# Splitting 8 KB weight tiles in one piece instead of two halves, with three buffers for each part

## The chip, the cores and the metric

The kernel runs on one core of a Trainium2 chip. The metric is the device time of one execution in microseconds, the median of three runs; lower is better.

## The reference, cut to what matters

The reference is two transformer-like blocks in float32 for one sequence of 256 tokens with 2048 channels. The first block computes six modulation vectors from a condition (`silu(c) @ w_ada + b_ada`), normalises and projects x, runs a state-space mixer and a dilated attention side by side, projects back, and adds a gated feed-forward layer. The second block has a neighbourhood attention, a latent attention, an attention over 256 memory tokens, and another feed-forward layer.

```python
mod = silu(c) @ w_ada + b_ada                    # 2048 -> 6 x 2048
proj = modulate(rms(x)) @ w_in                   # 256x2048 @ 2048x4096
x = x + gate1 * (concat(y_ssm, y_att) @ w_out)
x = x + gate2 * (silu(h2 @ w_gate) * (h2 @ w_up)) @ w_down
...
x = x + memory_attention(rmsnorm(x), rmsnorm(mem), w_xq, w_xk, w_xv, w_xo)
x = x + (silu(h @ w_gate_2) * (h @ w_up_2)) @ w_down_2
```

For the change only this matters: nearly all the work is products of 256 rows of activations with large float32 weight matrices, and each weight is used once.

## The kernel before, in words

**Weight tiles.** All weights come from HBM in tiles of 1 MB: 128 partitions by 4 chunks by 512 columns, 8 KB on each partition (four tiles have only 320 columns). `Flow.order` is a list, written out when the program is built, of all tiles in the order in which they are used. A tile of kind "w" is a matmul weight; a tile of kind "a" is a piece of `w_ada`. `Flow.run` walks the list. `feed` keeps up to six tiles ahead in the raw buffers `r` (L198, L199, issued from SyncE's queue). SyncE waits there until the VectorE work that last read the buffer is done.

**An "a" tile** is handed to `s_ada` (L948): one VectorE instruction of 128x2048 multiplies it by the condition and sums. There are 96 of them, mixed into the first part of the list, about one for each "w" tile at first and two for three later, until near 900 us.

**A "w" tile** is split in `split_half` into a part `h`, rounded to the matmul's format (fp32r) by a ScalarE copy (L207), and the rest `l = r - h` by a VectorE subtraction (L208). Before the change this is done for each half of a tile: two copies and two subtractions of 128x1024, into four buffers of 4 KB for `h` and four for `l`, so that two tiles fit. The argument `shared` would put the subtraction on GpSimd; `share` is `(0,)` everywhere, so it never does.

**The product** of a tile is in `mm3`: for each half, eight matmuls of 128x512 that use only `h` (L221 and L222, alternating), then four that use `l` (L226). So a tile is 24 matmuls, and TensorE needs the first `l` eight matmuls after the first `h`. `group` makes a loop of these over the tiles that add up in one accumulator, and hands the accumulator to a `done_*` task at its end.

**The order of the instructions** is that of the program text; nothing is reordered. Each engine executes its own instructions in that order. With two tiles split, `run` sends the older to `main` (its matmuls are issued) and then calls `step`, which advances every open task by one piece: evictions of accumulators (L875, L1227 on ScalarE, L871 and others on VectorE), transposes and further splits of activations (L262 to L264, L271 to L275), the state-space parameters and sections (L468 to L750), attention heads (L1090 to L1103), statistics (L291). So on each engine the order is: split of tile n+1, matmuls of tile n, tasks, split of tile n+2, matmuls of tile n+1, tasks. An "a" tile's L948 stands where the list has it, between two splits.

```python
split.append([])
for i in range(2):
    split[-1].append(k.split_half(r, i, ...))
    n += 1
    if n == k.NW:
        main.send(split.pop(0))
        self.step()
        n -= 2
```

Of the kernel before, what the change touches and what calls it, by code (L numbers as in the profile page):

```python
# [10 lines left out]
F32 = mybir.dt.float32  # L11
F32R = mybir.dt.float32r
AF = mybir.ActivationFunctionType
OP = mybir.AluOpType
# [136 lines left out]
class Core:  # L151
    NU = 40
    NU2 = 15
    NR, NW = 6, 4

    def __init__(self, ctx, tc):
        self.tc, self.nc = tc, tc.nc
        nc = self.nc

        def pool(name, **k):  # L160
            return ctx.enter_context(tc.tile_pool(name=name, bufs=1, **k))

        self.cp, self.wp, self.up, self.sp = pool("cp"), pool("wp"), pool("up"), pool("sp")
        self.pp = pool("pp", space=PSUM)
        self.dp = pool("dp", space=DRAM)
        self.n = 0
        self.ident = self.const([128, 128], "ident")
        make_identity(nc, self.ident)
        self.ones = self.const([128, 128], "ones")
        nc.gpsimd.memset(self.ones, 1.0)  # L170
        self.mhalf = self.const([128, 8], "mhalf")
        nc.gpsimd.memset(self.mhalf, -0.5)
# [26 lines left out]
        self.nc.sync.dma_start(r, src)  # L199
        return r  # L200

    def split_half(self, r, i, shared):

        nc = self.nc
        h, l = [self.wp.tile([128, 2, r.shape[-1]], F32R, name=self.nm(n), tag=n, bufs=self.NW) for n in "hl"]
        r = r[:, 2 * i:2 * i + 2]
        nc.scalar.activation(h, r, AF.Copy)  # L207
        (nc.gpsimd if shared else nc.vector).tensor_tensor(l, r, h.bitcast(F32), op=OP.subtract)  # L208
        return h, l

    def mm3(self, ps, acts, parts, first, last, ts=(0, 1)):

# [132 lines left out]
class Flow:  # L345


    def __init__(self, k):
        self.k = k
        self.order, self.fed, self.loaded = [], 0, []  # L350
        self.tasks = []
        self.ready = []
        self.lead = None
        self.share, self.nth = (0,), 0

    def add(self, task, rate=1):
        self.tasks.append([task, rate, 0.0])
# [25 lines left out]
    def run(self, main, other):  # L383

        k = self.k
        next(main)
        for g in other.values():
            next(g)
        split, n = [], 0
        for kind, _ in self.order:  # L390
            self.feed(k.NR)
            r = self.loaded.pop(0)
            if kind != "w":
                other[kind].send(r)
                continue
            split.append([])
            for i in range(2):
                split[-1].append(k.split_half(r, i, i >= 2 - self.share[self.nth % len(self.share)]))
                n += 1
                if n == k.NW:  # L400
                    main.send(split.pop(0))
                    self.step()
                    n -= 2
            if self.lead is not None:
                self.lead = next(self.lead, None) and self.lead
            self.nth += 1
        try:
            for p in split:
                main.send(p)
                self.step()  # L410
        except StopIteration:
            pass
        self.until(lambda: not self.tasks)
# [342 lines left out]
def build(ctx, tc, A, out):  # L756
    nc = tc.nc
    V, S, G, PE, SY = nc.vector, nc.scalar, nc.gpsimd, nc.tensor, nc.sync
    ctx.enter_context(tc.manual_schedule())
    k = Core(ctx, tc)  # L760
    fl = Flow(k)
# [84 lines left out]
    def group(acts, done, kbs, key=None, first=True, last=True, half=None):  # L846


        ps = open_ps.pop(key) if not first else [k.pm(), k.pm()] if half else k.pg()
        for i, kb in enumerate(kbs):  # L850
            parts = yield
            fl.until(lambda: kb in acts)
            end = last and i == len(kbs) - 1
            for ts in ((0,), (1,)) if half and end else ((0, 1),):
                for j in range(2):
                    k.mm3(ps, acts[kb][2 * j:2 * j + 2], parts[j], first and i == 0 and j == 0,
                          end and j == 1, ts)
                if half and end:
                    half(ps[ts[0]], ts[0])
        if half:  # L860
            return
        if last:
            fl.add(done(ps))
        else:
            open_ps[key] = ps
# [64 lines left out]
    def vals(g):  # L930
        def done(ps):
            o = tok(ps, r_mem)
            yield
            for t in range(2):
                SY.dma_start(mv[g][:, t], o[t])
        return done
# [51 lines left out]
    def s_norm1():  # L988
        for _ in range(6):
            yield  # L990
        for g in R4:
            load_x(g)
            yield
            yield
        for _ in range(4):
            yield
        for g in R4:
            row_stats(x[g], ss1, g)
            yield
        k.row_rstd(ss1, r1)  # L1000
        yield
        for g in R4:
            xs = scaled(g, r1)
            x[g] = [None, None]
            while (0, g // 2) not in got or (1, g // 2) not in got:
                yield
            acts1[g] = modulate(xs, g, 0)
            yield
# [122 lines left out]
    def s_prep():  # L1131
        yield from ssm.params()
        for s in range(NSEC):
            yield from ssm.prep(s)
        for _ in range(3):
            yield
        ssm.finish()
# [398 lines left out]
    def main():  # L1536
        prep = fl.add(s_prep(), 1)
        fl.add(s_norm1())
        yield from group(m_acts, keys(0), R4)
        fl.share = (0,)  # L1540
        prep[1] = 2
        for g in (1, 2, 3):
            yield from group(m_acts, keys(g), R4)
        for g in R4:
            yield from group(m_acts, vals(g), R4)
        m_acts.clear()
        fl.share = (0,)
        prep[1] = 3
        fl.add(s_run())
        fl.add(s_heads1())  # L1550
        done = {"u": done_u, "q": done_q, "k": done_k, "v": done_v}
        for n, g in EARLY:
            yield from group(acts1, hold((n, g % 2)), (0, 1))
        for n, g in EARLY:
            yield from group(acts1, done[n](g % 2), (2, 3))
        for n, g in LATE:
            yield from group(acts1, done[n](g % 2), R4)
        acts1.clear()
        for g in R4:
            yield from group(mixed_acts, out1(g, 0), (2,))  # L1560
        fl.share = (0,)
        for g in range(2):
            yield from group(glu_acts, done_glu(g), (0, 1))
        glu_acts.clear()
        for g in R4:
            yield from group(mixed_acts, out1(g, 1), (3,))
        for g in R4:
            yield from group(mixed_acts, out1(g, 2), (0, 1), half=(lambda ps, t: out1_end(3, ps, t)) if g == 3 else None)
        fl.until(lambda: not fl.tasks)
        ssm_scope.close()  # L1570
        pool2.append(ctx.enter_context(tc.tile_pool(name="pool2", bufs=1)))
        rope.append(pool2[0].tile([128, 2, 2, 32], F32, name="rope"))
        S.dma_start(rope[0], A["rope"].rearrange("p (a b c) -> p a b c", a=2, b=2))
        fl.share = (0,)
        fl.add(norm2())
        yield from ffn(acts2, None, fin1)
        acts2.clear()
        yield from group(acts3, done_cq, R4)
        yield from group(acts3, done_ckv, R4)
        fl.add(s_na())  # L1580
        fl.add(s_mla())
        for n in range(3):
            yield from group(acts3, done_qkv(n, 0), R4)
        for i in range(2):
            parts = yield
            fl.until(lambda: "ckv" in lat)
            for g in range(2):
                ps = k.pg()
                k.mm3(ps, lat["ckv"], parts[g], True, True)
                fl.add(done_ukv(i, g)(ps))  # L1590
        for g in (0, 2, 1):
            yield from group(cq_acts, done_uq(g), (0,))
        for n in range(3):
            yield from group(acts3, done_qkv(n, 1), R4)
        acts3.clear()
        for i in (1, 0):
            for g in R4:
                yield from group(y_acts, out2(i, g), (2 * i, 2 * i + 1))
        for g in R4:
            yield from group(acts4, done_xq(g), R4)  # L1600
        acts4.clear()
        seen = set()
        for g, kbs in XO:
            last = 3 in kbs
            yield from group(x_acts, out3(g), kbs, g, g not in seen, last)
            seen.add(g)
        x_acts.clear()
        for g in R4:
            fn.append(unit2())
            S.dma_start(fn[g], A["fnorm"][:, 512 * g:512 * g + 512].to_broadcast([128, 512]))  # L1610
        yield from ffn(acts5, r5, fin2, half2)
# [23 lines left out]
```

## Time and profile before

| | |
|---|---|
| median of 3 runs | 2713.08 us (2709.04 to 2713.55) |
| the profiled execution's own time | 2711.92 us |
| its span, first to last instruction | 2710.1 us |
| TensorE busy (matmuls) | 2616.3 us, 97% |
| VectorE busy | 1670.5 us, 62% |
| ScalarE busy | 1269.8 us, 47% |
| mean granted TensorE clock | 0.989 of full speed |

The page says what each engine did in one execution. A share over the whole span averages over stages that have different limits, so the rows below are mostly of stretches. In the rows PE is TensorE, DVE VectorE, ACT ScalarE, SP SyncE, and L208 is line 208 of the kernel before.

### The profile page before, as it was taken

What the parts mean: (1) busy time and instruction counts of PE and PEld (TensorE: products, weight loads), DVE (VectorE), ACT (ScalarE), POOL (GpSimd) and SP (SyncE); (2) the same over time, 40 slices, a digit from 0 to 9 for tenths busy, and PEclk for the clock granted to TensorE, in tenths of its full rate; (3) what the DMA queues carried; (4) which work ended last, traced back from release to release, by engine and by line L of the source; (5) the groups of instructions that cost most, each with busy time, mean ns of one, the idle gap of its engine ahead of it and who ended that gap; (6) DMA issues with size and microseconds to landing.
All of it is one profiled execution on the core that took longest, in us unless ns stands there. A gap on an engine that the chain in (4) does not pass through costs nothing.

```text
span 2710.1 us, 31194 instructions
## 1 busy us (share of the span) xinstructions
PE 2616.3 (97%) x12144; PEld 2171.3 (80%) x12144; DVE 1670.5 (62%) x2124; ACT 1269.8 (47%) x1818; POOL 98.6 (4%) x103
## 2 busy tenths in 40 slices
PE   8889989888999999999999999999999999999998
PEld 6778777776877888888888878888888888888887
DVE  7987999878766554554465454655554544455445
ACT  5465446553644344433445554555544433443434
POOL 2000000100000000000000021100000000000001
PEclk9999999999999999999999999999999999999999
DMA  8988765667676555555545434454455555555552
GB/s 348 362 289 328 307 244 215 253 225 297 256 277 232 200 196 190 186 194 195 186 168 192 171 130 162 166 200 171 178 215 197 186 189 196 191 186 186 187 198 96
DMA packets 90147, 578.98 MB, mean 214 GB/s; under 512 B 10000, under 2 KB 12432, under 8 KB 22672
## 3 DMA queue, kind: packets, MB, share of 16 engines
q1 hardware_dynamic: 80928, 561.61, 55.8%
q10 hardware_dynamic: 9072, 15.38, 1.7%
q8 instruction: 95, 1.56, 0.2%
q14 instruction: 52, 0.43, 0.0%
HBM read 570.67 MB, written 6.29 MB: 213 GB/s over the span
## 4 chain that ended last, share of the span: by engine, by line
PE 79%; DVE 15%; ACT 2%; issue 2%; DMA 1%; POOL 0%; ACTq 0%; DVEq 0%; POOLq 0%
PE g L226 24%; PE g L221 24%; PE g L222 24%; DVE l L208 4%; DVE r L948 4%; PE m L238 2%; DVE v L627 1%; ACT h L207 1%; DVE C L635 0%; PE m L342 0%; PE m L1484 0%; PE m L1471 0%; DVE u L732 0%; PE m L240 0%; PE m L226 0%
## 5 line engine op out<-in xcount | busy, mean ns | idle before, releaser
L208 DVE TENSOR_TENSOR l<-r,h 128x1024 fp32r<-128x1024 f32 x866 | 1028.5, 1223 | 573.6 <-ACT h L207 568.0
L221 PE MATMUL g<-h,u 128*128 128x512 f32 x3424 | 1352.6, 395 | 8.8 <-ACT h L207 6.5
L222 PE MATMUL g<-h,u 128*128 128x512 f32 x3424 | 1338.2, 391 | 0.0
L207 ACT ACTIVATE h<-r 128x1024 fp32r<-128x1024 f32 x866 | 884.1, 1056 | 625.1 <-PE g L222 593.0
L226 PE MATMUL g<-l,u 128*128 128x512 f32 x3424 | 922.2, 391 | 33.0 <-DVE l L208 33.0
L226 PEld LDWEIGHTS g<-l,u 128*128 128x128 f32 x3424 | 643.2, 189 | 178.3 <-DVE l L208 45.6
L221 PEld LDWEIGHTS g<-h,u 128*128 128x128 f32 x3424 | 647.9, 189 | 144.8 <-ACT h L207 10.2
L222 PEld LDWEIGHTS g<-h,u 128*128 128x128 f32 x3424 | 648.0, 189 | 132.4 <-issue 1.0
L948 DVE CUSTOM_DVE_ANT_0 r<-r,cond,vec 128x2048 f32<-128x2048 f32 x96 | 224.5, 2343 | 0.2
L271 ACT ACTIVATE u<-m 128x512 fp32r<-128x512 f32 (+1 forms) x80 | 42.7, 574 | 164.1 <-PE m L238 128.3
L272 DVE TENSOR_TENSOR u<-m,u 128x512 fp32r<-128x512 f32 (+1 forms) x80 | 50.0, 658 | 86.6 <-ACT u L271 86.5
L291 ACT ACTIVATE j<-u 128x512 bf16<-128x512 f32 (+2 forms) x92 | 47.3, 514 | 118.2 <-DVE u L1204 31.2
L238 PE MATMUL m<-ident,u 128*128 128x128 f32 x372 | 53.4, 287 | 19.8 <-POOL base_e L488 7.1
L274 ACT ACTIVATE u<-m,vec 128x256 fp32r<-128x256 f32 x86 | 38.9, 472 | 69.8 <-PE m L342 30.8
L275 DVE SCALAR_TENSOR_TENSOR u<-m,vec,u 128x256 fp32r<-128x256 f32 x86 | 40.0, 481 | 48.2 <-ACT u L274 48.1
L238 PEld LDWEIGHTS m<-ident,u 128*128 128x128 f32 x372 | 45.9, 148 | 27.5 <-ACT u L978 8.7
L299 POOL TENSOR_TENSOR r<-s,mhalf 128x2 f32<-128x2 f32 x5 | 5.5, 1102 | 1098.7 <-DVE s L298 1098.7
L1251 DVE TENSOR_TENSOR w<-g,w 128x512 f32<-128x512 f32 x24 | 16.5, 687 | 43.1 <-PE g L226 43.1
L1235 DVE SCALAR_TENSOR_TENSOR w<-g,r,w 128x512 f32<-128x512 f32 x22 | 15.5, 747 | 44.4 <-PE g L226 44.4
L1233 DVE TENSOR_TENSOR w<-g,w 128x512 f32<-128x512 f32 x22 | 14.2, 686 | 44.3 <-PE g L226 44.3
L1507 DVE TENSOR_TENSOR u<-g,u 128x512 f32<-128x512 f32 x22 | 14.2, 686 | 44.3 <-PE g L226 44.3
L1227 ACT ACTIVATE w<-g,r 128x512 f32<-128x512 f32 x22 | 13.9, 686 | 52.9 <-PE g L226 52.9
(238 smaller groups left out, 1204.6 us busy)
## 6 DMA issues: line engine op xcount, KB each, us to landing
r<-in_w_ada_dram SPq DMA_DIRECT2D x96, 1024.0 KB, 5.6
r<-in_wg_dram SPq DMA_DIRECT2D x88, 1024.0 KB, 4.8
r<-in_wu_dram SPq DMA_DIRECT2D x88, 1024.0 KB, 4.8
r<-in_wd_dram SPq DMA_DIRECT2D x88, 1024.0 KB, 4.8
r<-in_w_in_dram SPq DMA_DIRECT2D x32, 1024.0 KB, 6.0
r<-in_w_out_dram SPq DMA_DIRECT2D x32, 1024.0 KB, 4.8
r<-in_w_qkv_dram SPq DMA_DIRECT2D x24, 1024.0 KB, 4.8
r<-in_w_xk_dram SPq DMA_DIRECT2D x16, 1024.0 KB, 9.0
```

Source lines behind the costliest of these rows:

```text
L207: nc.scalar.activation(h, r, AF.Copy)
L208: (nc.gpsimd if shared else nc.vector).tensor_tensor(l, r, h.bitcast(F32), op=OP.subtract)
L221: nc.tensor.matmul(ps[t][:, :n], al[:, s], h[:, k], start=first and k == 0, stop=False)
L222: nc.tensor.matmul(ps[t][:, :n], ah[:, s], h[:, k], start=False, stop=False)
L226: nc.tensor.matmul(ps[t][:, :n], ah[:, s], l[:, k], start=False, stop=last and k == len(acts) - 1)
L238: self.nc.tensor.transpose(o, i, self.ident)
L271: nc.scalar.activation(h, ps, AF.Copy)
L272: nc.vector.tensor_tensor(l, ps, h.bitcast(F32), op=OP.subtract)
L274: nc.scalar.activation(h, ps, AF.Copy, scale=w)
L275: nc.vector.scalar_tensor_tensor(l, ps, w, h.bitcast(F32), op0=OP.mult, op1=OP.subtract)
L291: self.nc.scalar.activation(j[:, :n], src, AF.Square, accum_out=acc)
L948: V.tensor_tensor_reduce(r, r, cond, 1.0, v("b_ada", 8 * h + j), OP.mult, OP.add, md[h // 2][:, n:n + 1])
```

## The change

A tile is split whole: one ScalarE copy and one VectorE subtraction of 128x2048. `h` and `l` have three buffers of 8 KB each, where they had four of 4 KB. The two halves that `mm3` uses are slices of the whole tile, so the order of the matmuls is as before. `run` sends the older tile when two are split, at the same place as before. The unused `share` and `nth` go, and the scratch for GpSimd's descriptors is made smaller.

```diff
-    NR, NW = 6, 4
+    NR, NH, NL = 6, 3, 3
...
-    def split_half(self, r, i, shared):
+    def split_tile(self, r):
 
         nc = self.nc
-        h, l = [self.wp.tile([128, 2, r.shape[-1]], F32R, name=self.nm(n), tag=n, bufs=self.NW) for n in "hl"]
-        r = r[:, 2 * i:2 * i + 2]
+        h, l = [self.wp.tile([128, 4, r.shape[-1]], F32R, name=self.nm(n), tag=n, bufs=b)
+                for n, b in (("h", self.NH), ("l", self.NL))]
         nc.scalar.activation(h, r, AF.Copy)
-        (nc.gpsimd if shared else nc.vector).tensor_tensor(l, r, h.bitcast(F32), op=OP.subtract)
-        return h, l
+        nc.vector.tensor_tensor(l, r, h.bitcast(F32), op=OP.subtract)
+        return [(h[:, i:i + 2], l[:, i:i + 2]) for i in (0, 2)]
...
-            split.append([])
-            for i in range(2):
-                split[-1].append(k.split_half(r, i, i >= 2 - self.share[self.nth % len(self.share)]))
-                n += 1
-                if n == k.NW:
-                    main.send(split.pop(0))
-                    self.step()
-                    n -= 2
+            split.append(k.split_tile(r))
+            if len(split) == 2:
+                main.send(split.pop(0))
+                self.step()
...
-    nc = bacc.Bacc("TRN2", target_bir_lowering=False, num_devices=1, dynamic_dma_scratch_size=512)
+    nc = bacc.Bacc("TRN2", target_bir_lowering=False, num_devices=1, dynamic_dma_scratch_size=128)
```

## Rows read from the trace of the kernel before

**Rows 1.** The page, chain that ended last: shares of the span by engine.

```profile
PE 79%; DVE 15%; ACT 2%; issue 2%; DMA 1%; POOL 0%; ACTq 0%; DVEq 0%; POOLq 0%
```

**Rows 2.** Busy us by stretch: PE, PEld, DVE, ACT, POOL, then PEclk, DMA share, GB/s.

```profile
27.00:173.00 146.00, 132.48 (x604) 105.20 (x602) 141.93 (x273) 71.63 (x112) 9.40 (x6) 1.00 0.93 345
270.00:515.00 245.00, 221.29 (x1156) 186.52 (x1155) 236.91 (x455) 123.49 (x262) 17.66 (x10) 0.95 0.66 251
580.00:656.00 76.00, 66.51 (x286) 52.26 (x285) 75.86 (x87) 32.92 (x50) 0.00 (x0) 0.98 0.85 320
750.00:1400.00 650.00, 646.30 (x2892) 534.25 (x2891) 351.41 (x338) 274.26 (x310) 0.00 (x0) 1.00 0.55 202
```

**Rows 3.** The same columns (no POOL), only instructions on accumulator tile g.

```profile
750.00:1400.00 650.00, 635.90 (x2788) 522.08 (x2787) 26.62 (x40) 10.71 (x20) 1.00 0.55 202
```

**Rows 4.** Timeline, VectorE and TensorE, 112 to 119 us: start, length, engine, line.

```profile
112.57 2.34 DVE L948 CUSTOM_DVE_ANT_0 r<-r,cond,vec 128x2048 f32<-128x2048 f32 x1
114.84 2.35 DVE L208 TENSOR_TENSOR l<-r,h 128x1024 fp32r<-128x1024 f32 x2
...
116.11 1.19 PE L226 MATMUL g<-l,u 128*128 128x512 f32 x4 [1.93 <-DVE l L208]
```

**Rows 5.** Waits of TensorE, 0 to 1000 us: us in total, times, longest.

```profile
PE g L226 <- DVE l L208: 32.6, 28, 3.4
...
PE g L221 <- ACT h L207: 6.5, 4, 2.8
```

**Rows 6.** Groups by form, whole span: busy us, mean ns | idle before, releaser.

```profile
L208 DVE TENSOR_TENSOR l<-r,h 128x1024 fp32r<-128x1024 f32 x858 | 1022.4, 1226 | 571.3 <-ACT h L207 567.5 <-DMA r<-in_w_out_dram 0.8
L948 DVE CUSTOM_DVE_ANT_0 r<-r,cond,vec 128x2048 f32<-128x2048 f32 x96 | 224.5, 2343 | 0.2
...
L208 DVE TENSOR_TENSOR l<-r,h 128x640 fp32r<-128x640 f32 x8 | 6.2, 822 | 2.3 <-PE g L226 1.7 <-ACT h L207 0.5
...
L207 ACT ACTIVATE h<-r 128x1024 fp32r<-128x1024 f32 x858 | 878.7, 1059 | 622.6 <-PE g L222 590.5 <-DMA r<-in_w_in_dram 11.1 <-DMA r<-in_w_xk_dram 8.5
```

**Rows 7.** Line 208 in three stretches (27, 270 and 580 us): count, ns min/median/max.

```profile
L208 DVE TENSOR_TENSOR l<-r,h x44: 1215/1218/1224, 26.1 to 170.3; 128x1024 fp32r<-128x1024 f32 x44
...
L208 DVE TENSOR_TENSOR l<-r,h x55: 1211/1218/1226, 269.7 to 514.5; 128x1024 fp32r<-128x1024 f32 x55
...
L208 DVE TENSOR_TENSOR l<-r,h x22: 1210/1218/1223, 583.1 to 655.6; 128x1024 fp32r<-128x1024 f32 x22
```

**Rows 8.** Timeline of ScalarE, 7 to 11 us: an activation of 128x2048.

```profile
8.25 1.91 ACT L894 ACTIVATE cond<-cond 128x2048 f32<-128x2048 f32 x1 [5.31 <-DMA cond<-in_c_dram]
```

**Rows 9.** Chain that ended last, around 410, 653 and 371 us: start, length, what.

```profile
409.92 0.95 ACT h L207
...
410.90 2.36 DVE l L208 x2
...
653.06 0.96 ACT h L207
...
654.07 0.50 PE g L221
...
370.40 1.15 DVE l L208
...
371.59 2.07 PE g L226 x4
```

**Rows 10.** Timeline, 1929 to 1936 us: ScalarE, VectorE, TensorE.

```profile
1931.90 1.99 ACT L207 ACTIVATE h<-r 128x1024 fp32r<-128x1024 f32 x2
...
1932.97 2.36 DVE L208 TENSOR_TENSOR l<-r,h 128x1024 fp32r<-128x1024 f32 x2 [1.96 <-ACT h L207]
...
1934.94 1.07 PE L226 MATMUL g<-l,u 128*128 128x512 f32 x4
```

**Rows 11.** Waits of ScalarE and VectorE, 0 to 750 us: us in total, times, longest.

```profile
ACT h L207 <- PE g L222: 46.9, 33, 3.5
...
DVE l L208 <- ACT h L207: 22.3, 20, 3.8
```

More of the change, by code (lines that the diff above doesn't have):

```diff
@@ L353, in __init__ @@
         self.lead = None
-        self.share, self.nth = (0,), 0
     def add(self, task, rate=1):
@@ L388, in run @@
             next(g)
-        split, n = [], 0
+        split = []
         for kind, _ in self.order:
@@ L395, in run @@
                 continue
-            split.append([])
-            for i in range(2):
-                split[-1].append(k.split_half(r, i, i >= 2 - self.share[self.nth % len(self.share)]))
-                n += 1
-                if n == k.NW:
-                    main.send(split.pop(0))
-                    self.step()
-                    n -= 2
+            split.append(k.split_tile(r))
+            if len(split) == 2:
+                main.send(split.pop(0))
+                self.step()
             if self.lead is not None:
                 self.lead = next(self.lead, None) and self.lead
-            self.nth += 1
         try:
@@ L1539, in main @@
         yield from group(m_acts, keys(0), R4)
-        fl.share = (0,)
         prep[1] = 2
@@ L1546, in main @@
         m_acts.clear()
-        fl.share = (0,)
         prep[1] = 3
@@ L1560, in main @@
             yield from group(mixed_acts, out1(g, 0), (2,))
-        fl.share = (0,)
         for g in range(2):
@@ L1573, in main @@
         S.dma_start(rope[0], A["rope"].rearrange("p (a b c) -> p a b c", a=2, b=2))
-        fl.share = (0,)
         fl.add(norm2())
```

## The prediction

> **What bounds the kernel now.** I read the chain of waits first, since the busy shares mislead: TensorE is busy 97% of the span, but the chain gives it 79% and VectorE 15% [rows 1]. The table by stretch shows where that 15% lies. From 27 to 173 us VectorE is busy 141.93 of 146 us, from 270 to 515 us 236.91 of 245, from 580 to 656 us 75.86 of 76 [rows 2]. These stretches, 467 us together, go at VectorE's pace: for each weight tile it has one subtraction pair, mostly one L948, and tasks. From 750 to 1400 us TensorE is busy 646.3 of 650 us and VectorE about half [rows 2]; there a matmul of an accumulator takes 635.90 / 2788 = 0.228 us [rows 3], a tile of 24 about 5.5 us, and nothing that only VectorE or ScalarE saves can shorten it.
>
> The timeline shows how TensorE waits in the first kind of stretch: VectorE ends an L948, starts the pair at 114.84, and TensorE's first l matmul comes at 116.11, one half (1.2 us) later, after 1.93 us of idling [rows 4]. Up to 1000 us there are 28 such waits, 32.6 us together, and four for h, 6.5 us [rows 5].
>
> **The parts of the change, and what each costs.** The sum is made against the profiled execution's own 2711.92 us (span 2710.1), which is 1.2 us below the median of 2713.08. About 0.2%, 5.4 us, is what a measurement of this kernel can tell from no change.
>
> *One subtraction instead of two.* The trace has no subtraction of 128x2048. The two forms of L208 give a line: (1226 - 822) / 384 = 1.052 ns for a column [rows 6], so 1226 + 1024 x 1.052 = 2303 ns, near the 2343 ns of L948, which also reads two inputs of 128x2048 [rows 6]. A pair takes 2.35 us in the timeline [rows 4], not 2 x 1.226, because the second starts before the first has been written. So a tile saves 2.36 - 2.30 = 0.06 us of VectorE's time. That counts only where VectorE sets the pace: 44 + 55 + 22 = 121 halves, 60 tiles [rows 7], so 60 x 0.06 = 3.6 us are gained. The ends: at L948's price 0.01 us a tile and 1 us in all; at the bare slope, 2048 x 1.052 = 2.15 us, 0.2 us a tile and 12 us in all. I take the line through the same instruction's two sizes. The other tiles save the same behind TensorE, at no gain; TensorE's 5.5 us for a tile cover 2.3.
>
> *One copy instead of two.* An activation of 128x2048 takes 1.91 us [rows 8], a pair 1.99 [rows 10]: 0.08 us less for ScalarE, which is near half busy everywhere in [rows 2]. I take nothing for that. But h is now ready 1.91 us after the copy starts, and was ready for its first half after 1.06 [rows 6]: 0.85 us later. That costs where the chain goes from a first copy at once into VectorE or TensorE, as at 409.92 and 653.06 [rows 9]. I count six such places in the chain up to 656 us, at 279, 410, 434, 444, 539 and 653 us (the two shown stand for them): 6 x 0.85 = 5.1 us lost. At the low end ScalarE's queue has let it start earlier and nothing is lost; before these copies ScalarE came straight from other work, so I take the whole.
>
> *The first l comes with the second.* It is ready 2.30 us after the subtraction starts, and was after 1.226: 1.07 us later. In a stretch at VectorE's pace TensorE only waits longer at the first l and no longer behind it, and VectorE, which paces both, does not notice. The lateness is paid once, where the chain leaves VectorE by a first half for TensorE, as 370.40 to 371.59 [rows 9]; I find it again at 513: 2 x 1.07 = 2.1 us. The low end is nothing; the high end is the first rival.
>
> *Late in the kernel*, where TensorE sets the pace, a late part costs only what its slack doesn't cover. At 1931.90 the copy starts, h would end at 1933.81, l at 1936.11, and TensorE reads l at 1934.94: 1.2 us late [rows 10]. Four other places after 1400 us come out 0.5 to 1.2 us late by the same sum, but their copies and the third buffer leave some room; I take the widest one alone, 1.2 us, with ends 0 and 4.
>
> *The third buffer.* ScalarE waits for a free h 33 times up to 750 us, 46.9 us [rows 11]. These waits go. What is late next is the queue itself: the copy of tile n+2 stands behind the tasks that follow the matmuls of tile n, some of which wait for those matmuls. VectorE waits for h only 22.3 us in 20 places [rows 11], and in its three stretches it is 97 to 100% busy, so an earlier copy only lies longer in its buffer. I take nothing; the second rival says what it could bring.
>
> *SyncE and the rest.* A raw buffer is given back when the subtraction of its whole tile is done, within 0.06 us of where it was, so the loads start as before. The send of the older tile, the tasks and the matmuls keep their places. GpSimd's smaller scratch issues and moves nothing.
>
> The sum: 2711.9 - 3.6 + 5.1 + 2.1 + 1.2 = 2716.7, say **2717 us**, 0.14% over the median. The pieces nearly cancel, so the likeliest single answer is no change that can be told.
>
> **The rivals.**
>
> *The late first part is paid at every wait* (slower). If within a tile's time VectorE comes to wait for something behind those l matmuls on TensorE's queue (a transposition of a task, an accumulator), each of the 28 waits [rows 5] hands its 1.07 us back to VectorE: 28 x 1.07 = 30 us, less the 3.6, so about 2738 us; at half the waits 2723. The granted clock, 0.95 from 270 to 515 us [rows 2], could fall further with longer idling. It decides from the point where VectorE's own work for a tile is shorter than TensorE's with the longer wait. Against it: VectorE has only 4.1, 8.1 and 0.1 us idle in the three stretches [rows 2], so it seldom waits for anybody. For it: after 750 us, in each stage where ScalarE's slack is short, the same happens. The Trainium skill, Perfetto Trace Analysis (Optimizing Scalar/DVE Operations), says that where these engines aren't saturated but leave others with bubbles, breaking instructions up may complete work sooner; this change does the opposite, and by the rows of TensorE's waits that rule would hold here if VectorE were not full.
>
> *The third buffer gives a tile of lead* (faster). If ScalarE and VectorE enter each of the three stretches one tile further ahead, TensorE has 5.5 us more to live on in each: 3 x 5.5 = 16 us, so about 2701. For it: 39 us of TensorE's waits are for h and l [rows 5]. Against it: the tasks in the queues, as above, and a lead is used up only once in a stretch that VectorE paces.
>
> *Merging saves the whole fixed time of an instruction.* By the line of L208 that is 1226 - 1024 x 1.052 = 149 ns [rows 6]; 60 x 0.149 = 8.9 us instead of 3.6, and 2711.4 us. The Trainium skill, VectorE: DVE Perf Modes (The TRN2 errata), has a single large tile pay a fixed cost once where small ones pay it each time. The pair at 2.35 us [rows 4] speaks against it: most of that fixed time lies under the next instruction.
>
> That the change doesn't do what it says (copies that still come one buffer late) would leave the sum without its third buffer, which is the forecast itself.
>
> **How the numbers follow.** The forecast, terms that nearly cancel, 0.52, with 2708 to 2724 as its own range from the ends of its terms; the late part paid often, 0.20 (2723 to 2744); a tile of lead, 0.18 (2690 to 2708); the whole fixed time saved, 0.10 (about 2711). Faster by over 0.2% (under 2707.7): the lead case and little else, 0.20. Slower by over 0.2% (over 2718.5): the first rival and a third of the forecast's own range, 0.37. Within: 0.43. The range of 2698 to 2732 takes the ends of the forecast, most of the lead case and half of the first rival, and leaves out about 2 in 10.
>
> **What would show it.** Right: L208 at 2.30 us and L207 at 1.91 for 128x2048; up to 656 us about as many waits of TensorE for l, each up to 1 us longer where VectorE is full; VectorE's busy time down by about 433 x 0.06 = 26 us (433 tiles are the 858 + 8 halves of [rows 6]), nearly all of it behind TensorE; ScalarE's waits for TensorE at L207 mostly gone. Wrong: VectorE with many idle microseconds in its three stretches (first rival); TensorE's waits for l well under 30 us and the stage before 660 us shorter (second); or new waits for h or l in several stages after 750 us.

## The result, and the profile after

The changed kernel takes 2733.99 us (median of four runs, 2730.18 to 2738.65) beside 2712.93 us before: a ratio of 1.0085, 95% interval 1.0073 to 1.0097. It is slower by about 22 us (21 between the two medians, 23 by the ratio). The forecast was 2717 us, no change that can be told, with a range up to 2732; it was wrong. The profiled execution took 2730.18 us, the shortest of the four, and has the highest mean granted clock of them (0.992; the others 0.987 to 0.989); its span is 2728.4 us.

The prices came out as read from the rows. The groups by form of the changed kernel (busy us, mean ns | idle before, releaser; its line numbers are those of before in the split, the matmuls and the splits of activations, and 6 lower in the tasks shown, so that L942 is L948):

```profile
L208 DVE TENSOR_TENSOR l<-r,h 128x2048 fp32r<-128x2048 f32 x429 | 971.3, 2290 | 527.2 <-ACT h L207 527.0
...
L207 ACT ACTIVATE h<-r 128x2048 fp32r<-128x2048 f32 x429 | 810.7, 1915 | 424.5 <-PE g L222 375.9 <-DMA r<-in_w_in_dram 19.4 <-DVE mod L942 5.7
```

The whole subtraction takes 2290 ns (2303 were estimated in [rows 6]), the whole copy 1915 ns (1910 in [rows 8]). In the timeline the answer to [rows 4] is this, VectorE first, then TensorE's first l matmul of the same tile:

```profile
112.26 2.35 DVE L942 CUSTOM_DVE_ANT_0 r<-r,cond,vec 128x2048 f32<-128x2048 f32 x1
...
114.53 2.29 DVE L208 TENSOR_TENSOR l<-r,h 128x2048 fp32r<-128x2048 f32 x1
...
116.87 1.20 PE L226 MATMUL g<-l,u 128*128 128x512 f32 x4 [1.85 <-DVE l L208]
```

The first l matmul comes 2.34 us after the subtraction starts, where it came after 1.27; TensorE's wait is 1.85 us, where it was 1.93 [rows 4], so here it is not even longer. VectorE paces this stretch, and a later first l costs nothing in it, as forecast. The busy time by stretch (columns as in [rows 2]) shows what became of VectorE:

```profile
27.00:173.00 146.00, 132.88 (x600) 105.89 (x598) 141.72 (x253) 68.53 (x90) 9.77 (x7) 0.99 0.93 348
270.00:515.00 245.00, 213.52 (x1142) 178.73 (x1140) 233.19 (x427) 117.44 (x233) 17.67 (x10) 0.98 0.67 251
580.00:656.00 76.00, 65.26 (x279) 50.65 (x278) 74.63 (x75) 30.43 (x37) 0.00 (x0) 0.98 0.86 325
```

It idles 4.3, 11.8 and 1.4 us in the three stretches, together 5.2 us more than before [rows 2]: the small saving of the merged instruction was waited away. The waits of TensorE up to 1000 us, answering [rows 5], and of VectorE up to 750 us, answering [rows 11] (us in total, times, longest):

```profile
PE g L226 <- DVE l L208: 39.2, 33, 3.8
PE g L221 <- ACT h L207: 11.5, 7, 2.5
...
DVE l L208 <- ACT h L207: 33.3, 24, 3.9
```

TensorE waits 11.6 us more there, VectorE 11 us more for h. But where are the 22 us? The start of the first matmul of a tile, taken from the two traces, tells it: a tile's number is its place in the list, and the difference to before is the time lost up to it.

```
tile    start before   start after   lost so far
  30        222.1 us      218.7 us      -3.4 us
  89        710.7         714.1         +3.4
 204       1352.9        1356.4         +3.5
 306       2000.4        2018.7        +18.3
 432       2695.7        2714.0        +18.3
```

14.8 of the profiled execution's 18.3 us are lost between 1353 and 2000 us, in the stages where TensorE sets the pace and where I had put 1.2. This is easily overlooked, for TensorE's listed waits from 1380 to 2030 us are short (us in total, times, longest):

```profile
PE g L226 <- DVE l L208: 4.5, 11, 2.4
PE g L221 <- ACT h L207: 2.6, 6, 0.9
```

A matmul follows the last one by 0.227 us, but is shown 0.39 us long, so a gap of up to 0.16 us does not show as a wait, and the first matmul after a gap is followed more slowly.

A part of the 14.8 us is the clock. The stretch from 1540 to 1590 us in the changed kernel, TensorE in it, and the same stretch before:

```profile
1540.00:1590.00 50.00, 44.79 (x209) 36.83 (x208) 25.01 (x25) 28.87 (x50) 8.96 (x10) 0.93 0.40 137
...
1579.01 1.97 PE L226 MATMUL g<-l,u 128*128 128x512 f32 x4 [2.38 <-DVE l L208]
...
1540.00:1590.00 50.00, 45.02 (x220) 37.05 (x219) 25.76 (x35) 32.55 (x62) 11.78 (x13) 1.00 0.40 139
```

The granted clock is 0.93 here, where it was 1.00 before (1.00 too from 1360 to 2010 us). By these numbers TensorE lost about 50 x 0.07 = 3.5 us to the lower of its two levels, an estimate. It stood at that level twice, from 1552 and from 1579 us. Ahead of the first it had idled 2.00 us for ScalarE's L869, as at the same place before, where the clock did not fall; ahead of the second it had idled 2.38 us for a late l. The other three kernels below that subtract these tiles whole, with two tiles split ahead, show 0.93 or 0.94 in this stretch; those with halves in their order show 1.00. So by this estimate some 11 of the 14.8 us are the lateness itself, and some 3.5 come with it by the clock.

One of the late places, from the chain that ended last of the changed kernel:

```profile
1379.19 2.29 DVE l L208
1381.48 0.41 DVE u L275
...
1381.91 0.48 ACT u L274
...
1382.42 0.89 DVE u L275 x2
...
1383.33 0.47 ACT u L274
1383.81 1.81 ACT h L207
...
1385.64 2.30 DVE l L208
...
1387.99 1.21 PE g L226 x4
```

This is the thing to see. The late subtraction of one tile holds VectorE's next task (L275, a split of activations); that task and ScalarE's L274 answer each other in turn; and ScalarE's copy of the next tile stands behind them in its queue. The lateness of one tile is handed on to the next, and then the next is late by its own size as well. The same place in the trace of before, VectorE, then ScalarE, then TensorE's first matmul with the h of the next tile (timeline):

```profile
1374.88 2.36 DVE L208 TENSOR_TENSOR l<-r,h 128x1024 fp32r<-128x1024 f32 x2 [1.80 <-ACT h L207]
1377.16 0.48 DVE L275 SCALAR_TENSOR_TENSOR u<-m,vec,u 128x256 fp32r<-128x256 f32 x1
...
1373.80 1.99 ACT L207 ACTIVATE h<-r 128x1024 fp32r<-128x1024 f32 x2
...
1379.46 3.90 ACT L207 ACTIVATE h<-r 128x1024 fp32r<-128x1024 f32 x4
...
1381.91 0.39 PE L221 MATMUL g<-h,u 128*128 128x512 f32 x1
```

And in the changed kernel:

```profile
1377.26 1.90 ACT L207 ACTIVATE h<-r 128x2048 fp32r<-128x2048 f32 x1
...
1383.70 3.71 ACT L207 ACTIVATE h<-r 128x2048 fp32r<-128x2048 f32 x2
```

From one copy's start to the next it was 1379.46 - 1373.80 = 5.66 us and is 1383.70 - 1377.26 = 6.44: 0.78 us more before the second copy even starts. To this come 0.85 us of the longer copy, and for l 1.06 us of the longer subtraction.

### The profile page after: what moved, and what is told of

Read it like the earlier page. It is cut to its first block, busy times and chain, and to the rows that moved or that the text cites. A ratio compares the mean times of both kernels' runs of the same rounds, so it can differ in the third digit from the quotient of the medians.

```text
span 2728.4 us, 29776 instructions
## 1 busy us (share of the span) xinstructions
PE 2617.6 (96%) x12144; PEld 2163.0 (79%) x12144; DVE 1619.9 (59%) x1691; ACT 1200.9 (44%) x1385; POOL 98.8 (4%) x103
## 4 chain that ended last, share of the span: by engine, by line
PE 76%; DVE 16%; ACT 5%; issue 2%; DMA 1%; POOL 0%; ACTq 0%; DVEq 0%; POOLq 0%
PE g L226 24%; PE g L221 23%; PE g L222 23%; DVE l L208 6%; DVE r L942 4%; ACT h L207 2%; PE m L238 1%; DVE u L275 1%; DVE v L621 1%; ACT j L291 0%; PE m L342 0%; PE m L1478 0%; PE m L1465 0%; DVE C L629 0%; ACT u L274 0%
## 5 line engine op out<-in xcount | busy, mean ns | idle before, releaser
L208 DVE TENSOR_TENSOR l<-r,h 128x2048 fp32r<-128x2048 f32 x433 | 977.1, 2282 | 528.9 <-ACT h L207 528.6
L207 ACT ACTIVATE h<-r 128x2048 fp32r<-128x2048 f32 x433 | 815.4, 1909 | 424.5 <-PE g L222 375.9
L942 DVE CUSTOM_DVE_ANT_0 r<-r,cond,vec 128x2048 f32<-128x2048 f32 x96 | 224.6, 2344 | 0.2
L271 ACT ACTIVATE u<-m 128x512 fp32r<-128x512 f32 (+1 forms) x80 | 42.7, 575 | 256.2 <-PE m L238 220.7
L274 ACT ACTIVATE u<-m,vec 128x256 fp32r<-128x256 f32 x86 | 38.9, 473 | 79.9 <-DVE u L275 34.4
L1227 DVE TENSOR_TENSOR w<-g,w 128x512 f32<-128x512 f32 x22 | 14.2, 686 | 83.0 <-PE g L226 83.0
L275 DVE SCALAR_TENSOR_TENSOR u<-m,vec,u 128x256 fp32r<-128x256 f32 x86 | 39.9, 481 | 33.6 <-ACT u L274 33.4
L1221 ACT ACTIVATE w<-g,r 128x512 f32<-128x512 f32 x22 | 13.9, 686 | 98.7 <-PE g L226 98.7
L1221 ACT ACTIVATE w<-g 128x512 f32<-128x512 f32 x22 | 12.0, 596 | 102.7 <-PE g L226 102.7
```

Source lines behind the costliest of these rows:

```text
L208: nc.vector.tensor_tensor(l, r, h.bitcast(F32), op=OP.subtract)
L271: nc.scalar.activation(h, ps, AF.Copy)
L274: nc.scalar.activation(h, ps, AF.Copy, scale=w)
L275: nc.vector.scalar_tensor_tensor(l, ps, w, h.bitcast(F32), op0=OP.mult, op1=OP.subtract)
L942: V.tensor_tensor_reduce(r, r, cond, 1.0, v("b_ada", 8 * h + j), OP.mult, OP.add, md[h // 2][:, n:n + 1])
```

## The experiments

Two theories. **A**: lateness. The whole copy and the whole subtraction are ready later, and VectorE's later end holds tasks and through them the next copy. **B**: the buffers. Three whole tiles instead of four halves let the splits stand elsewhere in time, and the queues meet in a worse way. For each kernel below the time lost up to tile 30, 89, 204 and 306, read as above from its profile, is in the table at the end of this section.

**Halves in three whole buffers.** The changed kernel, with two copies and two subtractions again:

```diff
-        nc.scalar.activation(h, r, AF.Copy)
-        nc.vector.tensor_tensor(l, r, h.bitcast(F32), op=OP.subtract)
+        for i in (0, 2):
+            nc.scalar.activation(h[:, i:i + 2], r[:, i:i + 2], AF.Copy)
+        for i in (0, 2):
+            nc.vector.tensor_tensor(l[:, i:i + 2], r[:, i:i + 2], h[:, i:i + 2].bitcast(F32), op=OP.subtract)
```

> Three whole-tile buffers for h and l as in the changed kernel, but two copies and two subtractions of 128x1024 for a tile as before. Theory A (the size of the instruction: the whole copy and the whole subtraction come late, and hold the tasks behind them): the loss goes, about 2712 us, and from 1380 to 2030 us of before's time nothing is lost against before. Theory B (the buffers: three whole tiles let the splits stand elsewhere and the queues meet differently): about 2734 us as in the changed kernel. If the third buffer was worth a tile of lead, under 2706 us.

Measured: 2711.83 us beside 2711.34, ratio 1.0001 (0.9992 to 1.0011). The whole loss is gone, so B falls. It also shows that the third buffer is worth nothing: at each tile of the table its matmuls stand within 0.2 us of where they were, but for 1 us gained at the start. ScalarE's waits, in this kernel (its edit shifts the lines: L208, L273 and L1223 here are L207, L271 and L1227 before):

```profile
ACT h L208 <- PE g L224: 355.3, 106, 3.4
ACT u L273 <- PE m L240: 218.1, 26, 10.2
ACT w L1223 <- PE g L228: 198.5, 21, 9.8
```

and before:

```profile
ACT h L207 <- PE g L222: 593.0, 390, 3.5
ACT u L271 <- PE m L238: 128.3, 26, 5.7
ACT w L1227 <- PE g L226: 108.7, 21, 5.3
```

ScalarE's waits for a free h fall by 238 us, and its waits in the tasks that stand next in its queue grow by 180 in the two groups shown alone. The waits moved along the queue; nothing became earlier for TensorE. It also speaks against a third theory, that VectorE gives a raw buffer back later and so the loads start later: ScalarE waits 36.9 us for loads of `r` up to 750 us here, where nothing is lost, and 32.3 us in the changed kernel.

**The whole split in two buffers.** The edit is `NR, NH, NL = 6, 2, 2`.

> The changed kernel with two whole buffers for h and two for l instead of three. Theory A: the copy of a tile now also waits until the matmuls of the tile two before it are done with both halves, so it is later still: 2740 to 2765 us. Theory B (the third buffer does the harm): back to about 2715 us. If the third buffer has no effect at all: 2734 us.

Measured: 2735.79 us, ratio 1.0085 (1.0068 to 1.0102), the same as with three. A's price for the missing buffer was a miss; with the run before it, the third buffer has no effect with either size.

**The copy in halves, the subtraction whole.**

```diff
-        nc.scalar.activation(h, r, AF.Copy)
+        for i in (0, 2):
+            nc.scalar.activation(h[:, i:i + 2], r[:, i:i + 2], AF.Copy)
```

> The changed kernel with the copy in two halves again and the subtraction whole. Theory A with the lateness handed on by VectorE: l ends as late as in the changed kernel (two copies of 2.0 us, then 2.28), so most of the loss stays, 2728 to 2736 us, and TensorE's waits for h go while those for l stay or grow. A theory in which only the late h costs: about 2716 us.

Measured: 2734.72 us, ratio 1.0083 (1.0068 to 1.0098). An early first h alone gives nothing back. TensorE's waits from 1380 to 2030 us went over from h to l (L209 is the subtraction, L208 the copy):

```profile
PE g L227 <- DVE l L209: 11.6, 12, 2.5
...
PE g L222 <- ACT h L208: 0.3, 1, 0.3
```

**The copy whole, the subtraction in halves.** The other half of that edit.

> The changed kernel with the copy whole and the subtraction in two halves again. Theory A: the first l comes 1.06 us earlier than in the changed kernel, but VectorE ends the tile no sooner and h is as late; TensorE's waits for l shrink, those for h stay: 2720 to 2728 us. A theory in which only the late first l costs: about 2714 us; one in which only the late h costs: 2734 us.

Measured: 2728.35 us, ratio 1.0062 (1.0047 to 1.0077). An early first l gives back some 6 us, just short of what was expected. The single edits give back 0 and 6 us, both together 22. So neither part is to blame alone: what both together change, and neither alone does, is when VectorE is done with the tile, because a subtraction that waits for both copies ends late whether it is one instruction or two.

**Lateness without long instructions.** Three kernels with the halves of the first experiment, that only turn the order of the halves round. The edit is `(2, 0)` for `(0, 2)` in the loop of the copies, in that of the subtractions, or in both.

> Everything in halves of 128x1024 with three whole-tile buffers, but ScalarE copies the second half first; VectorE still subtracts the first half first, so it waits for both copies. Instructions are as short as before; the first h is 0.95 us late, the first l 0.95 us late, VectorE ends the tile 0.9 us late. If lateness is what costs: 2725 to 2732 us, as with the copy whole and the subtraction in halves (2728). If the length of the instructions as such costs: 2712 us.

Measured: 2730.01 us, ratio 1.0071 (1.0054 to 1.0087).

> Everything in halves; the copies in order, but VectorE subtracts the second half first, so it starts only after both copies and the first l comes last. The first h is in time, the first l about 2 us late, VectorE's end 0.9 us late: the times of the kernel with the copy in halves and the subtraction whole. If lateness costs: 2730 to 2738 us. If the length of the instructions as such costs: 2712 us.

Measured: 2742.11 us, ratio 1.0116 (1.0101 to 1.0131), a little over what was expected.

> Everything in halves, both engines take the second half first. The first h is 0.95 us late and the first l 1.1 us late for TensorE, but VectorE starts after one copy and ends the tile as early as before. If the loss is handed on by VectorE (its late end holds the tasks, which hold the next copy): 2712 to 2718 us, and no loss after 1380 us. If only the late arrival at TensorE counts: 2725 to 2732 us, as with the copies alone turned round.

Measured: 2718.32 us, ratio 1.0027 (1.0017 to 1.0038), just over the first range. Short instructions lose as much as long ones when they are late, so length as such is not what costs. The first and the third of these kernels bring h and l to TensorE at about the same late time (0.95 to 1.1 us late, worked out from the lengths of the instructions); the third frees VectorE 0.9 us sooner, and loses 3.2 us between tiles 204 and 306 where the first loses 13.5. So most of the lateness is handed on by VectorE. The 3.2 us that are left were not expected; a part may be the clock (0.97 from 1540 to 1590 us there), the rest the late arrival by itself. In the traces, VectorE with the copies alone turned round (L210 is the subtraction, L277 the split L275):

```profile
1381.01 2.36 DVE L210 TENSOR_TENSOR l<-r,h 128x1024 fp32r<-128x1024 f32 x2 [2.75 <-ACT h L208]
1383.29 0.48 DVE L277 SCALAR_TENSOR_TENSOR u<-m,vec,u 128x256 fp32r<-128x256 f32 x1
...
1387.62 4.63 DVE L210 TENSOR_TENSOR l<-r,h 128x1024 fp32r<-128x1024 f32 x4 [1.41 <-ACT h L208]
```

and with both:

```profile
1377.95 2.36 DVE L210 TENSOR_TENSOR l<-r,h 128x1024 fp32r<-128x1024 f32 x2 [1.80 <-ACT h L208]
1380.22 0.48 DVE L277 SCALAR_TENSOR_TENSOR u<-m,vec,u 128x256 fp32r<-128x256 f32 x1
...
1383.61 4.63 DVE L210 TENSOR_TENSOR l<-r,h 128x1024 fp32r<-128x1024 f32 x4 [0.47 <-ACT h L208]
```

VectorE's idling before the first pair is 2.75 us with the copies alone, and 1.80 with both, as before the change; before the next tile it is 1.41 and 0.47.

**The early and the late stages apart.** The size of copy and subtraction is chosen by the tile's number `nt`: whole for `nt < 89`, up to about 710 us, in one kernel, and whole for `nt >= 89` in the other.

> The first 89 tiles (up to about 710 us) are split whole, the others in halves, three whole-tile buffers throughout. If the stages add: the loss up to 710 us alone, 2714 to 2721 us, and nothing is lost after it. If the early stage loses what the late ones lose, over 2725 us.

Measured: 2723.07 us beside 2711.70, ratio 1.0047 (1.0032 to 1.0062), between the two theories' ranges.

> The complement of the run with the first 89 tiles whole: here the first 89 are in halves and all later tiles are split whole, two ahead, three whole-tile buffers. If the two parts add: the 14.8 us that the changed kernel loses between 1353 and 2000 us of before's time and nothing else, 2724 to 2728 us. If a late stage loses less when it is entered without the early loss: under 2720 us.

Measured: 2723.66 us beside 2711.63, ratio 1.0049 (1.0033 to 1.0066). So about 11 us are lost in the early part and 12 in the late one, and the two add up to the whole loss. In the profile of the second kernel the late loss is 14.3 us. The early loss differs from execution to execution: 3.4 us in the changed kernel's profile, 8.3 in that of the first of these two, whose instructions are the same up to tile 89. The mean granted clock up to 715 us is 0.98 in the one and 0.96 in the other (0.96 before too), so in the changed kernel's profile, its fastest execution, the clock likely hides a part of the early loss. The late loss hardly differs (14.8 and 14.3). In the first of the two kernels VectorE's idle time in the three stretches is 4.9, 13.9 and 3.9 us:

```profile
27.00:173.00 146.00, 133.84 (x605) 106.80 (x604) 141.11 (x250) 69.65 (x91) 9.40 (x6) 0.99 0.92 345
270.00:515.00 245.00, 217.34 (x1141) 182.44 (x1140) 231.11 (x425) 118.27 (x232) 15.09 (x10) 0.95 0.66 251
580.00:656.00 76.00, 66.82 (x284) 52.74 (x284) 72.15 (x74) 31.04 (x38) 0.00 (x0) 0.96 0.85 328
```

The first stretch lost nothing (2.3 us gained by tile 30); the loss is in the second and third and in the stages between. That the attention heads and the state-space sections, whose tasks go to and fro between ScalarE and VectorE there, hand the lateness on is likely, but was not followed.

**The whole subtraction only where it cannot hurt.** Halves everywhere, except the subtraction of tiles 4 to 29.

> Halves everywhere, except that the subtraction is whole for tiles 4 to 29, in the first stretch that VectorE paces; three whole-tile buffers. Theory: in that stretch the late first l costs nothing and 26 tiles save 0.06 to 0.07 us of VectorE each, 1.7 us, so 2708 to 2712 us, the same as before within what can be told. If even there the late l costs: 2714 us or more.

Measured: 2709.36 us beside 2711.01, ratio 0.9996 (0.9987 to 1.0006). It is not to be told from before; the 1.7 us that it should save are below what a run can show. Nothing that was tried is faster than before beyond its interval.

**Splitting three tiles ahead.** The one line that decides how many tiles are split before the oldest goes to the matmuls, `if len(split) == 2:`, becomes `if len(split) == 3:`, in the changed kernel and in the one with halves.

> The changed kernel with the tile sent to the matmuls when three are split, not two, so that the split of a tile stands one tile earlier in the queues and the third buffer is used. Theory (lateness handed on, and a third buffer that the order of the queues leaves without use): a tile's 5.5 us cover the 2 us of lateness, nothing is lost from 1380 to 2030 us and the waits for h up to 750 us go: 2700 to 2716 us. If TensorE's waits come from something that the earlier split does not move: 2728 to 2736 us.

Measured: 2730.95 us, ratio 1.0076 (1.0061 to 1.0091). The gain that was expected did not come.

> The same order, three tiles split ahead, with the split in halves. Theory: nothing is late in the later stages anyway, so what is left to gain is in the stage up to 750 us, where VectorE's work for a tile now stands ahead of the tasks of the tile before: 2695 to 2712 us. If the tasks, held up by a tile, cost more than the lead gives: 2715 to 2730 us.

Measured: 2730.37 us, ratio 1.0073 (1.0056 to 1.0090). The time is the same for both sizes, and the parts differ from those of all other kernels: from tile 204 to 306 the whole split now loses 2.5 us instead of 14.8, so a tile of lead that stands in the queues does cover the lateness; but up to tile 89 both lose 16 to 20 us. The likely reason, argued from the queues, is that each task now stands behind one more split; the mean granted clock up to 715 us is also lower (0.93 and 0.92, before 0.96), and its part is not separated from that of the tasks. The stretch from 515 to 580 us with whole tiles three ahead shows it:

```profile
515.00:580.00 65.00, 48.38 (x215) 39.86 (x214) 45.66 (x84) 33.19 (x67) 3.67 (x1) 0.74 0.57 206
```

TensorE is busy 48.4 of 65 us, and its granted clock is 0.74, about half of the time at the lower of its two levels (1.2 instead of 2.4 GHz). Before, the same stretch was

```profile
515.00:580.00 65.00, 55.97 (x288) 47.13 (x288) 42.00 (x73) 41.07 (x86) 0.00 (x0) 0.90 0.54 205
```

TensorE waits more for the tasks, up to 760 us first in the kernel three ahead (L737 there is L743 before, where this wait was 3.8 us, three times):

```profile
PE m L737 <- DVE u L730: 11.0, 6, 3.9
PE g L226 <- DVE l L208: 10.9, 10, 2.0
PE m L238 <- ACT u L972: 10.8, 5, 7.3
```

Its waits for l fell from 39.2 us to 10.9, and others took their place.

The time lost against before up to four tiles, in the profile of each kernel:

```
                                     tile 30    89      204     306
changed kernel                         -3.4    +3.4    +3.5   +18.3
halves in three whole buffers          -1.1    -1.0    -1.0    -0.9
whole, two buffers                     -2.4    +9.7   +11.3   +25.6
copy in halves, subtraction whole      -3.0    +3.4    +5.0   +21.6
copy whole, subtraction in halves      -0.7    +4.9    +4.9   +14.4
copies second half first               -0.4    +5.2    +5.2   +18.7
subtractions second half first         -1.0   +14.2   +14.2   +30.6
both second half first                 -1.8    +3.1    +3.1    +6.3
whole up to tile 89                    -2.3    +8.3   +10.0   +10.0
whole from tile 89                     -2.0    -2.6    -2.6   +11.7
whole subtraction, tiles 4 to 29       -4.9    -5.0    -5.0    -5.0
whole, three ahead                     +3.8   +19.7   +19.7   +22.2
halves, three ahead                    +3.5   +16.1   +17.7   +17.1
```

## Why the prediction was wrong

**The prices of the instructions** were right: 2290 ns and 1915 ns, and VectorE's busy time fell from 1670.5 to 1619.9 us. That is 51 us, twice the 26 that I had named, and it bought nothing. The likely reason, worked out and not tried: back to back, a pair takes 2.36 us and merging saves 0.06 or 0.07; where the two subtractions stood apart, each waiting for its own h, merging saves 2 x 1.226 - 2.290 = 0.16 us, and there VectorE idles before each anyway (571 us in all before L208 in [rows 6]). The rival that merging saves an instruction's whole fixed time had the price of one instruction right and the pair wrong, as argued. The Trainium skill, VectorE: DVE Perf Modes (The TRN2 errata), gives (N + 151) / 0.96 ns for a float32 addition of two tensors, 2291 ns for 2048. The trace agrees for this subtraction, with 2290 ns.

**"Late in the kernel"** is the step that failed. I took each copy's start from the trace of before, added the longer copy and the longer subtraction once, and found one place 1.2 us late, at most 4 us in all. The start itself moves: 0.78 us in the place shown, since the tile before ends late on VectorE, and the tasks between answer each other on two engines. So at 1381 us h, with 1.39 us of slack before (1380.52 to 1381.91 us), came 0.78 + 0.85 = 1.63 us later, and l followed. The term measured 14.8 us in the profile (14.3 alone, 12 us between medians), twelve times what I took; some 3.5 us of it are the granted clock, for which the term had nothing. I did not ask which instruction stands behind the subtraction in VectorE's queue, and who waits for that.

**"One copy instead of two" and "the first l comes with the second"**, the early terms, had the mechanism and not the size: -3.6 + 5.1 + 2.1 = 3.6 us were summed, 11.4 us were measured by the kernel with the first 89 tiles whole (8.7 to 16.8 by its interval). I counted six places where the chain of before enters by a copy; the waits show VectorE waiting for h 11 us longer up to 750 us, at 24 places instead of 20. With two tiles split ahead these waits are 31 to 40 us in every kernel above whose early subtractions all wait for both copies, and 17 to 23 us in all others. Which of these places carry the rest of the early loss was not settled tile by tile, since the granted clock falls at other places in each execution; so this part of the cause is argued, and its size alone is measured.

**The first stretch** (27 to 173 us) went as forecast: VectorE full, TensorE's later first l for free.

**"The third buffer"** at nothing was right, and more than I claimed: with halves 238 us of waits at L207 vanish and no matmul of the table moves by it. Up to 750 us they went as said (46.9 us before, 7.3 in the changed kernel); over the whole span 375.9 us of 593.0 stayed, so they did not mostly go. The rival that it gives a tile of lead falls. It also needed the order of the queues changed, and then the early part lost more.

**"SyncE and the rest"** had a raw buffer given back within 0.06 us of where it was. Where VectorE waits for both copies it is given back later, 0.78 us at the place shown; that this did not cost much by the loads is what the waits of the kernel with halves in three buffers speak for.

**"The late first part is paid at every wait"** had the sign and nearly the time, but the price at the wrong place, so that the time is luck in part. It counted TensorE's 28 waits up to 1000 us; those grew by 6.6 us in all, and more than half of the loss is after 1380 us, where [rows 5] has no row. Its last argument, that the same happens after 750 us where ScalarE's slack is short, named that place without a price, and the sign of being wrong that went with it came true: 11 waits for l and 6 for h from 1380 to 2030 us, where the trace of before lists a single one, of 0.5 us for l. The Trainium skill, Perfetto Trace Analysis (Optimizing Scalar/DVE Operations), says that breaking up instructions of engines that are not full may let work be completed sooner where they leave others with bubbles; in the late stages VectorE and ScalarE are about half busy, and the runs agree: 2711.83 us with halves and 2733.99 with whole tiles.

## What to carry to other kernels

When an instruction that feeds the bound engine gets longer, follow its end and not only its result: the next instruction in its queue, who waits for that, and whether this chain leads back to the next feed. A buffer more gives no lead where the order of the queues, not the buffer, decides when the work is issued; a wait that disappears there turns up at the next instruction. And a cheap test of "late" against "long" is to turn the order of two halves round.

## What had not been expected of the hardware

Gaps on TensorE of less than 0.16 us are invisible in its waits, because a matmul of 128x512 is shown 0.39 us long and starts 0.227 us after the one before. After the gap at 1385.66 us the next matmul came 0.33 us later instead of 0.227 (timeline of TensorE in the changed kernel):

```profile
1384.49 1.07 PE L226 MATMUL g<-l,u 128*128 128x512 f32 x4
1385.66 0.50 PE L221 MATMUL g<-h,u 128*128 128x512 f32 x1
1385.99 0.40 PE L222 MATMUL g<-h,u 128*128 128x512 f32 x1
1386.23 0.40 PE L221 MATMUL g<-h,u 128*128 128x512 f32 x1
```

So 7.1 us of listed waits for h and l from 1380 to 2030 us stood beside a loss of 14.8: some 3.5 us of the difference are the clock, and the rest lies in gaps too short to be listed and in matmuls that follow a gap late. Why the subtractions turned round alone (2742 us) lose 7 us more than one whole subtraction at nearly the same times (2735) stays open; most of the difference is up to tile 89, where the granted clock is also lower (0.95 up to 715 us, beside 0.97).
